# Sample tokens through ScalarE's DMA queue, sums of x held behind x, and separate banks for the second value tile, in a hybrid mLSTM and attention layer

## Chip, cores and metric

One core of one Trainium2 chip. The metric is the device time of one execution in microseconds (us). Engines: PE is TensorE (matmuls and transposes; PEld its weight loads), DVE is VectorE, ACT is ScalarE, POOL is GpSimd, SP is SyncE, which issues most DMAs. 0.3% of this kernel's time is 7.5 us.

## The reference

One inference step of one decoder layer. 512 prompt tokens and 32 sample tokens (8 sequences of 4), each a row of 2048 numbers, go through the same layer:

```
u = x @ w_in                      # 2048 x 18952, split into q,k,v,o,z (mLSTM), q,k,v,z (attention), two gates, ig, fg
h_m = mlstm(q_m, k_m, v_m, ig, logsigmoid(fg))      # 4 heads of 512, with a carried state C, n, m
h_a = sliding_window_attention(q_a, k_a, v_a)       # 32 heads of 64 over 4 key/value heads, window 128, sinks
br_m = norm(h_m) * sigmoid(o_m) * silu(z_m);  br_a = h_a * silu(z_a)
y = sigmoid(g_m) * (br_m @ w_proj_m) + sigmoid(g_a) * (br_a @ w_proj_a)
out = layernorm(2**0.25 * x + y @ w_out)
```

All is float32. Besides `out` for both groups of tokens, the new states C, n, m and the new key and value buffers are returned.

## The kernel before

**Products.** The 544 tokens (512 + 32) are the columns of the moving operand, in two halves of 272; 128 columns of a weight are the stationary one. A float32 product is made of three products in the faster fp32r form: a number is split into a high part (a cast to fp32r by ScalarE) and a low part (the difference, by VectorE), and high times high, high times low and low times high are summed. `split` (L190 to L198) does this for a loaded weight half, 128 partitions of 8 × 128: `wh` on ScalarE, `wl` on VectorE. `hilo` (L237) does it for x. A weight half is a tile `raw`, loaded by `load_half` (L185) on SP's queue, and `wh` and `wl` have two buffers each.

**Plain tiles.** `gemm` (L219) makes one block of 128 output columns from 16 blocks k of 128 rows of x: 16 × 3 × 2 = 96 products (L205) into two PSUM banks of the pool `bank` (4 buffers). Only the attention's value columns, two such blocks `VA_` (kk = 0 and 1, L572 to L583), are made so, and the gates' 8 columns (`gates_half`, L364 to L382, twice 32 products at L381). The gates' halves stand before each half of kk = 1.

**Paired tiles.** All later blocks go two at a time through `paired` (from L643), a scheme in the manner of Strassen and Winograd: seven products of quarter size in place of eight. Each step has 24 products (16 with `wh`, L643, and 8 with `wl`, L645), and one of seven moving operands: quadrants of x (`a11`, `xk`) or sums of quadrants (`s1`, `n2`, `n3`, `s4`), each as a high and a low tile (`s1h`, `s1l` and so on). `prepare` adds raw weight quadrants (L623, on VectorE) and splits them, three steps ahead; `gather` takes results out of the banks into `ev` tiles.

**The start.** After a first load of constants come 20 warm-up transposes (L288). x is loaded by SP in five pieces of 256, 256, 512, 512 and 512 columns (L296), with weight halves of the value tiles between them. The sample tokens (`xs`, L302) are two loads of 32 × 1024 on SP's queue, behind the second piece of x and the first weight half. The loop from L310 takes the 16 blocks k: 4 transposes (L315) into a tile of the pool `sm` (4 buffers), whose contents are then cast and differenced into `a11`, `a21` (k below 8) or `xk` (k from 8). At k = 2 the sample tokens are turned too, in 16 transposes of 32 × 32 (L319) into one tile `pxs`, which is read out after every second pair of blocks (L332 to L338). For k below 8 ScalarE also copies the block into `n2r` and `s1r` (L323, L324); for k from 8 VectorE subtracts the copy from the new block (L328, and L338 for the sample tokens): this makes s1. n3 is formed at L342. `x_sums` (L538 to L562) then does the rest: n2 = n2r − s1r in four chunks (L541), `hilo` of n3, s1 and n2 in four chunks each, and, once the plain tiles are done, s4. Each chunk is 128 × 544.

**Order.** Each engine runs its instructions in one fixed order. A scheduler chooses that order when the kernel is built, from a simulated timeline in which each instruction has an estimated cost; `tc.high_priority` moves instructions ahead, and `tc.issue_after(ins)` holds an instruction behind `ins` on the engine that runs `ins`. Side work (`x_sums`, gates, `attn_values`) is written as generators, taken a step further at every `tick()`.

```
for kk in range(2):
    ps = gemm(win, VA_ + kk * 128, xh, xl, ..., every=4, prio=500 * kk, before=gates_between if kk else None)
    if kk == 0:
        sums_ = x_sums(); spawn(sums_); gates_ps = mm()
```

With four `bank` buffers, kk = 0 holds two and the gates two, so that kk = 1 gets its two when ScalarE has copied out those of kk = 0 (`ev`, L582).

Of the kernel before, what the change touches and what calls it, by code (L numbers as in the profile page):

```python
# [15 lines left out]
F32 = mybir.dt.float32  # L16
F32R = mybir.dt.float32r
AF = mybir.ActivationFunctionType
ALU = mybir.AluOpType

D = 2048
SEQ = 512
NB = 8
NTS = 4
NS = NB * NTS
T = SEQ + NS
KT = D // 128
# [46 lines left out]
def _build(tc, nc, i, o, es):  # L74
# [11 lines left out]
    V, A, G, PE = nc.vector, nc.scalar, nc.gpsimd, nc.tensor  # L86
# [13 lines left out]
    def nm(s):  # L100
        count[0] += 1
        return f"{s}_{count[0]}"

    def sm():
        return psB.tile([128, 512], F32, tag="sm", name=nm("sm"))
# [4 lines left out]
    def r32(ap):  # L110
        return ap.bitcast(F32)
# [4 lines left out]
    def blk(ap, n=4):  # L116
        return ap.rearrange("p (b x) -> p b x", b=n)
# [7 lines left out]
    state = {}  # L125
# [17 lines left out]
    ident = cc[:, C_ID:C_ID + 128]  # L143
# [41 lines left out]
    def load_half(wv, c0, half):  # L185
        raw = wr.tile([128, 8, 128], F32, tag="raw", name=nm("raw"))
        load_part(raw, wv, c0, half)
        return raw

    def split(raw, p=None, tags=("wh", "wl"), parts=1):  # L190
        p = p or wp
        wh = p.tile([128, 8, 128], F32R, tag=tags[0], name=nm("wh"))
        wl = p.tile([128, 8, 128], F32R, tag=tags[1], name=nm("wl"))
        n = 8 // parts
        for k in range(0, 8, n):
            A.copy(wh[:, k:k + n], raw[:, k:k + n])  # L196
            V.tensor_tensor(out=wl[:, k:k + n], in0=raw[:, k:k + n], in1=r32(wh[:, k:k + n]), op=ALU.subtract)  # L197
        return wh, wl  # L198
# [11 lines left out]
    EVEN = ((0, 0, 272), (1, 272, 272))  # L210

    def bank():
        return psA.tile([128, 512], F32, tag="bank", name=nm("bank"))

    def mm():

        return [bank(), bank()]

    def gemm(wv, c0, xh, xl, cols=EVEN, raws=(None, None), every=8, prio=0, before=None, parts=(1, 1)):  # L219
        ps = mm()  # L220
        for half in range(2):
            if before:
                before(half)
            raw = raws[half] or load_half(wv, c0, half)
            if prio:
                with tc.high_priority(offset=prio):
                    wh, wl = split(raw, parts=parts[half])
            else:
                wh, wl = split(raw, parts=parts[half])
            products(ps, half, wh, wl, xh, xl, cols, every)  # L230
        return ps
# [5 lines left out]
    def hilo(src, hi, lo, eng=None):  # L237
        A.copy(hi, src)
        (eng or V).tensor_tensor(out=lo, in0=src, in1=r32(hi), op=ALU.subtract)
# [10 lines left out]
    HT = T // 2  # L250
# [14 lines left out]
    xh, xl = xview(0), xview(1)  # L265
# [4 lines left out]
    wr2 = pool(esQ, "wr2", 3)  # L270
# [7 lines left out]
    n2r = tx.tile([128, 8, HT], F32, name="n2r")[:]  # L278
    s1r, n3r = (act2.tile([128, 8, HT], F32, tag="act", name=nm("r"))[:] for _ in range(2))

    def two_k(ch):
        return slice(ch * 2, ch * 2 + 2)

    xs_src = i["x_sample"].rearrange("b t d -> (b t) d")
    xp_src = i["x_prompt"][0].rearrange("(t p) d -> p t d", p=128)
    warm = sm()
    for _ in range(20):
        PE.transpose(warm[:, 0:128], ident, ident)  # L288
    raw0, xt, xs = [], [], []
    for c0, n in ((0, 256), (256, 256), (512, 512), (1024, 512), (1536, 512)):  # L290
        if c0 < 1536:
            t_ = xr.tile([128, 4, n], F32, tag=f"x{n}", name=nm("xr"))[:]
        else:
            t_ = act2.tile([128, 8, HT], F32, tag="act", name=nm("xr"))[:].rearrange("p a b -> p (a b)")
            t_ = blk(t_[:, 0:4 * n])
        xdma = nc.sync.dma_start(t_, xp_src[:, :, c0:c0 + n])  # L296
        xt += [t_[:, :, c:c + 128] for c in range(0, n, 128)]
        if c0 == 256:
            raw0.append(load_half(win, VA_, 0))
            for c in range(0, D, 1024):  # L300
                xs_ = wr2.tile([128, 8, 128], F32, tag="raw2", name=nm("xs"))
                nc.sync.dma_start(xs_[:NS].rearrange("p a b -> p (a b)"), xs_src[:, c:c + 1024])  # L302
                xs += [xs_[:NS, q] for q in range(8)]
        elif c0 == 1024:
            raw0.append(load_half(win, VA_, 1))
    state["load"] = xdma
# [2 lines left out]
    pxs = sm()  # L309
    for g in range(8):  # L310
        for q in range(2):
            k = g * 2 + q
            pt = sm()
            for t in range(4):
                PE.transpose(pt[:, t * 128:t * 128 + 128], xt[k][:, t], ident)  # L315
            if k == 2:

                for k_ in range(KT):
                    PE.transpose(pxs[:, k_ * 32:k_ * 32 + 32], xs[k_], ident[:NS, :NS])  # L319
            if k < 8:  # L320
                hilo(pt[:, 0:HT], a11[0][:, k], a11[1][:, k])
                hilo(pt[:, HT:SEQ], a21[0][:, k, 0:SEQ - HT], a21[1][:, k, 0:SEQ - HT])
                A.copy(n2r[:, k], pt[:, 0:HT])  # L323
                A.copy(s1r[:, k, 0:SEQ - HT], pt[:, HT:SEQ])  # L324
            else:
                hilo(pt[:], xk2[0][k // 4 - 2][:, k % 4, 0:SEQ], xk2[1][k // 4 - 2][:, k % 4, 0:SEQ])
                c = (slice(None), k - 8, slice(0, SEQ - HT))
                V.tensor_tensor(out=s1r[c], in0=pt[:, HT:SEQ], in1=s1r[c], op=ALU.subtract)  # L328
        if g % 2:
            k4 = slice((g // 2) * 4, (g // 2) * 4 + 4)  # L330
            src = blk(pxs[:, k4.start * 32:k4.stop * 32])
            if g < 4:  # L332
                hilo(src, *(a21[p][:, k4, SEQ - HT:HT] for p in range(2)))
                A.copy(s1r[:, k4, SEQ - HT:HT], src)
            else:
                hilo(src, *(xk2[p][g // 2 - 2][:, :, SEQ:T] for p in range(2)))
                c = (slice(None), slice(k4.start - 8, k4.stop - 8), slice(SEQ - HT, HT))
                V.tensor_tensor(out=s1r[c], in0=src, in1=s1r[c], op=ALU.subtract)  # L338
        if g == 3:
            for ch in range(4):  # L340
                ks_ = two_k(ch)
                V.scalar_tensor_tensor(n3r[:, ks_], n2r[:, ks_], -1.0, s1r[:, ks_], op0=ALU.mult, op1=ALU.subtract)  # L342
# [182 lines left out]
    def attn_keys(kk, kt):  # L525
# [9 lines left out]
        nc.sync.dma_start(kb_p[0].rearrange("t k d -> t (k d)")[:, cs], kr[:, 0:128])  # L535
        nc.sync.dma_start(d_ks[:, cs], kr[:32, 128:256])

    def x_sums():  # L538
        for ch in range(4):
            ks_ = two_k(ch)  # L540
            V.tensor_tensor(out=n2r[:, ks_], in0=n2r[:, ks_], in1=s1r[:, ks_], op=ALU.subtract)  # L541
            if ch % 2:
                yield
        for name, r_ in (("n3", n3r), ("s1", s1r), ("n2", n2r)):
            h_, l_ = S[name] = quad(act2, name)
            for ch in range(4):
                ks_ = two_k(ch)
                hilo(r_[:, ks_], h_[:, ks_], l_[:, ks_])
                if ch % 2:
                    yield  # L550

        while not state.get("plain_done"):
            yield
        s4 = S["s4"] = quad(act, "s4")
        for ch in range(4):
            ks_ = two_k(ch)
            k0 = (ch * 2) % 4
            h12, l12 = (r32(xk2[p][ch // 2][:, k0:k0 + 2, 0:HT]) for p in range(2))
            V.tensor_tensor(out=n2r[:, ks_], in0=h12, in1=n2r[:, ks_], op=ALU.subtract)
            V.tensor_tensor(out=n2r[:, ks_], in0=n2r[:, ks_], in1=l12, op=ALU.add)  # L560
            hilo(n2r[:, ks_], s4[0][:, ks_], s4[1][:, ks_])
            yield  # L562
# [8 lines left out]

    for kk in range(2):  # L572
        ps = gemm(win, VA_ + kk * 128, xh, xl, raws=((raw0[0], raw0[1]), (raw0[2], None))[kk], every=4, prio=500 * kk,
                  before=gates_between if kk else None)
        if kk == 0:
            sums_ = x_sums()
            spawn(sums_)
            gates_ps = mm()
        vt = ev()
        with ahead_of_sums():  # L580
            for p_, v_ in halves(ps, vt):
                A.copy(v_, p_)  # L582
        spawn(attn_values(kk, vt))  # L583
# [873 lines left out]
    for ct in range(16):  # L1457
        sg = c5t()
        nc.sync.dma_start(sg[:], d_sga[ct])
        ps = gemm(wa_, ct * 128, bah, bal, every=2)  # L1460
# [3 lines left out]
        if bmh is None and (not live or ct == 15):  # L1464
# [8 lines left out]
            wr2, pe_ = pool(esR, "wr2b", 3), pool(esR, "peb", 1)  # L1473
# [99 lines left out]
    wr2, pe_ = pool(esR, "wr2d", 3), pool(esR, "ped", 1)  # L1573
# [3 lines left out]
    for ct in range(4):  # L1577
        ps = gemm(wo, ct * 128, yh, yl, every=4, prio=AHEAD)
# [168 lines left out]
    raws = [load_half(wo, ct * 128, half) for ct, half in ((12, 0), (12, 1), (13, 0))]  # L1747
# [12 lines left out]
    ps = gemm(wo, 12 * 128, yh, yl, cols=CUT, prio=AHEAD, raws=raws[:2])  # L1760
# [5 lines left out]
    for g in range(G3):  # L1766
        ct = 16 - G3 + g
        ps = sm()
        raws = [raws[2] if (g, half) == (0, 0) else load_half(wo, ct * 128, half) for half in range(2)]
# [66 lines left out]
```

## Time and profile before

| | us |
|---|---|
| median of 3 runs | 2510.77 (2508.2 to 2514.76) |
| profiled execution, own time | 2505.34 |
| its span in the trace | 2503.5 |
| mean granted clock of PE | 0.996 |

The profile is of one execution. Its page begins with each engine's busy time and share. Other views ask the trace for more: a table by stretches of time; the groups of like instructions; the waits of an engine, with the engine, line and tile that ended them; and the timeline, whose rows give the start, the duration, the engine, the line, the operation, output<-inputs with their shape and the count, and in brackets the idle time before the row and what ended it. The duration of a matmul row reaches to its modelled end, which overlaps the next; the distance between starts is what a matmul costs.

### The profile page before, as it was taken

How to read it: one execution, taken by the hardware profiler on the slowest of the kernel's cores; microseconds unless marked ns; L12 is line 12 of the kernel's file. 1: busy time of each engine (PE TensorE's matmuls, PEld its weight loads, DVE VectorE, ACT ScalarE, POOL GpSimd, SP SyncE). 2: the span in 40 equal slices, each digit the busy share in tenths (PEclk: the TensorE clock that was granted, in tenths of full speed). 3: DMA queues.
4: the chain of work that ended last, by engine and by line, in shares of the span. 5: the costliest groups of instructions: out<-in, count | busy, mean ns of one | idle time of the engine just before them, and what ended most of it. 6: DMA issues, size and time to landing. Idle time of an engine off the chain costs nothing.

```text
span 2503.5 us, 48635 instructions
## 1 busy us (share of the span) xinstructions
PE 2476.5 (99%) x19562; PEld 2413.9 (96%) x19562; DVE 1814.0 (72%) x2783; ACT 1240.0 (50%) x2026; POOL 383.5 (15%) x370
## 2 busy tenths in 40 slices
PE   8999999999999999999999999999999999999997
PEld 8999999999999999999999999999999999999997
DVE  7867777777677677887777778777866654767667
ACT  5457676677677665443433444444633323344431
POOL 0211211211121120221112122211000000110101
PEclk9999999999999999999999999999999999999999
DMA  6776666666666645467576566566755546788776
GB/s 169 179 186 156 152 150 165 149 152 166 149 147 164 155 116 146 118 209 229 174 222 216 170 202 213 177 212 217 246 179 166 183 141 211 209 230 258 213 217 194
DMA packets 551089, 457.35 MB, mean 183 GB/s; under 512 B 44784, under 2 KB 451232, under 8 KB 550576
## 3 DMA queue, kind: packets, MB, share of 16 engines
q1 hardware_dynamic: 534160, 394.99, 52.7%
q0 software_dynamic: 15696, 57.15, 11.7%
q8 instruction: 154, 2.52, 0.4%
q10 hardware_dynamic: 1008, 2.10, 0.2%
q14 instruction: 71, 0.58, 0.1%
HBM read 313.82 MB, written 94.22 MB: 163 GB/s over the span
## 4 chain that ended last, share of the span: by engine, by line
PE 90%; issue 4%; DMA 2%; DVE 2%; ACT 0%; POOL 0%; SPq 0%; DVEq 0%; POOLq 0%; ACTq 0%
PE bank L643 45%; PE bank L645 22%; PE bank L205 9%; PE sm L1340 2%; PE sm L1159 1%; PE sm L1153 1%; PE sm L1372 1%; PE sm L751 1%; PE sm L1385 1%; PE sm L789 1%; PE sm L779 1%; PE sm L1702 1%; DMA raw<-in_w_out 1%; DMA raw<-in_w_in 0%; DVE wl L197 0%
## 5 line engine op out<-in xcount | busy, mean ns | idle before, releaser
L196 ACT CAST wh<-raw 128x1024 fp32r<-128x1024 f32 x632 | 661.9, 1048 | 822.8 <-PE bank L643 675.4
L197 DVE TENSOR_TENSOR wl<-raw,wh 128x1024 fp32r<-128x1024 f32 x632 | 780.6, 1236 | 266.9 <-ACT wh L196 226.5
L643 PE MATMUL bank<-xk,wh 128*128 128x272 f32 x2336 | 321.8, 288 | 0.7 <-DVE ev L668 0.7
L623 DVE TENSOR_TENSOR raw<-raw,raw 128x1024 f32<-128x1024 f32 x238 | 302.3, 1272 | 10.3 <-DMA raw<-in_w_in 4.9
L643 PEld LDWEIGHTS bank<-xk,wh 128*128 128x128 f32 x2336 | 303.6, 188 | 4.3 <-ACT wh L196 2.1
L662 POOL TENSOR_TENSOR ev<-p,ev 128x272 f32<-128x272 f32 x82 | 122.3, 1491 | 608.8 <-ACT ev L661 536.6
L645 PE MATMUL bank<-xk,wl 128*128 128x272 f32 x1168 | 173.5, 288 | 0.0
L643 PE MATMUL bank<-s1h,wh 128*128 128x272 f32 x656 | 170.0, 290 | 0.7 <-ACT wh L196 0.7
L643 PE MATMUL bank<-n3l,wh 128*128 128x272 f32 x656 | 169.6, 290 | 0.0
L643 PE MATMUL bank<-s4h,wh 128*128 128x272 f32 x656 | 169.3, 289 | 0.1
L643 PE MATMUL bank<-n3h,wh 128*128 128x272 f32 x656 | 169.3, 289 | 0.0
L643 PE MATMUL bank<-n2l,wh 128*128 128x272 f32 x656 | 169.0, 290 | 0.0
L643 PE MATMUL bank<-s1l,wh 128*128 128x272 f32 x656 | 168.8, 290 | 0.0
L643 PE MATMUL bank<-n2h,wh 128*128 128x272 f32 x656 | 168.7, 288 | 0.0
L643 PE MATMUL bank<-s4l,wh 128*128 128x272 f32 x656 | 168.6, 290 | 0.0
L645 PEld LDWEIGHTS bank<-xk,wl 128*128 128x128 f32 x1168 | 156.8, 188 | 0.1
L643 PE MATMUL bank<-a11l,wh 128*128 128x272 f32 x584 | 150.1, 290 | 0.0
L643 PE MATMUL bank<-a11h,wh 128*128 128x272 f32 x584 | 149.9, 288 | 0.0
L205 PE MATMUL bank<-bh,wl 128*128 128x272 f32 x704 | 148.2, 289 | 0.4 <-DVE wl L197 0.4
L205 PE MATMUL bank<-bh,wh 128*128 128x272 f32 x704 | 147.8, 290 | 0.0
L205 PE MATMUL bank<-bl,wh 128*128 128x272 f32 x704 | 147.3, 288 | 0.0
L621 POOL DMA_DIRECT2D raw<-raw x90 | 78.1, 868 | 310.6 <-DVE sums L764 153.1
(460 smaller groups left out, 5622.3 us busy)
## 6 DMA issues: line engine op xcount, KB each, us to landing
raw<-in_w_in SPq DMA_DIRECT2D x296, 512.0 KB, 4.3
raw<-raw POOLq DMA_DIRECT2D x90, 512.0 KB, 4.9
C<-in_state_mlstm_C SPq DMA_DIRECT2D x32, 1024.0 KB, 5.6
out<-C SPq DMA_DIRECT2D x64, 512.0 KB, 3.5
raw<-in_w_proj_a SPq DMA_DIRECT2D x32, 512.0 KB, 4.5
raw<-in_w_proj_m SPq DMA_DIRECT2D x32, 512.0 KB, 4.2
raw<-in_w_out SPq DMA_DIRECT2D x32, 512.0 KB, 4.6
d_sgm<-ev SPq DMA_DIRECT2D x16, 272.0 KB, 5.7
```

The source lines that it names most:

```text
L196: A.copy(wh[:, k:k + n], raw[:, k:k + n])
L197: V.tensor_tensor(out=wl[:, k:k + n], in0=raw[:, k:k + n], in1=r32(wh[:, k:k + n]), op=ALU.subtract)
L205: PE.matmul(ps[f][:, :w], a[:, kk], b(k, c, w), start=(k == 0 and n == 0), stop=(k == 15 and n == 2))
L621: G.dma_start(out=w[out][:], in_=w[b][:], accum_op=ALU.add)
L623: V.tensor_tensor(out=w[out][:], in0=w[a][:], in1=w[b][:], op=ALU.add)
L643: PE.matmul(ps, wh[:, k], x(p, k), start=(first and k == 0 and p == 0), stop=False, skip_group_check=True)
L645: state["end"] = PE.matmul(ps, wl[:, k], x(0, k), start=False, stop=(k == 7), skip_group_check=True)
L662: G.tensor_tensor(out=c22, in0=p1, in1=c11, op=ALU.subtract)
L751: PE.matmul(pp[:, c0 + w0:c0 + 256], qs[a][:, j * 128:j * 128 + 128], kx[:, k0:k0 + 256 - w0], start=(n == 0), stop=(n == 1))
L779: PE.transpose(pt[:, (m - m0_) * 128:(m - m0_) * 128 + 128], s_[:, b, 128:256] if own else s_[:, b + 1, 0:128], ident)
L789: PE.matmul(po[:, b * 128:b * 128 + n], VA[:, b], p_[:, 2 * b:2 * b + n // 128], start=(b == 0 and m == 0), stop=(b == 3 and m == 1), skip ...
L1340: PE.matmul(pp[:, 0:258], a[:, b * 128:b * 128 + 128], b_[:, b, f], start=(b == 0 and n == 0), stop=(b == 3 and n == 2))
```

## The change

1. The sample tokens are loaded by four DMAs of 32 × 512 that ScalarE's queue issues ahead of everything, each into 32 partitions of one 128 × 512 tile. They are turned in 4 transposes of 128 × 128 instead of 16 of 32 × 32; `pxs` is the same afterwards except for the order of its columns, which the reads from it follow.
2. The last subtraction of L328 (the end of x) is remembered, and in `x_sums` the subtraction of n2 and the `hilo` of n3, s1 and n2 are put behind it by `issue_after`. As that instruction is VectorE's, this binds the VectorE parts (n2, and the low tiles); ScalarE's casts are not bound.
3. The second value tile (kk = 1) accumulates in two `sm` tiles in place of two `bank`s.

```diff
-    def gemm(wv, c0, xh, xl, cols=EVEN, raws=(None, None), every=8, prio=0, before=None, parts=(1, 1)):
-        ps = mm()
+    def gemm(wv, c0, xh, xl, cols=EVEN, raws=(None, None), every=8, prio=0, before=None, parts=(1, 1),
+             ps=None):
+        ps = ps or mm()
...
-    raw0, xt, xs = [], [], []
+    raw0, xt = [], []
+    xs = wr2.tile([128, 8, 128], F32, tag="raw2", name=nm("xs"))
+    for q in range(4):
+        nc.scalar.dma_start(xs[q * 32:q * 32 + 32, 0:4].rearrange("p a b -> p (a b)"), xs_src[:, q * 512:q * 512 + 512])
...
-            for c in range(0, D, 1024):
-                xs_ = wr2.tile([128, 8, 128], F32, tag="raw2", name=nm("xs"))
-                nc.sync.dma_start(xs_[:NS].rearrange("p a b -> p (a b)"), xs_src[:, c:c + 1024])
-                xs += [xs_[:NS, q] for q in range(8)]
...
             if k == 2:
-                for k_ in range(KT):
-                    PE.transpose(pxs[:, k_ * 32:k_ * 32 + 32], xs[k_], ident[:NS, :NS])
+                for c in range(4):
+                    PE.transpose(pxs[:, c * 128:c * 128 + 128], xs[:, c], ident)
...
-                V.tensor_tensor(out=s1r[c], in0=pt[:, HT:SEQ], in1=s1r[c], op=ALU.subtract)
+                state["x_end"] = V.tensor_tensor(out=s1r[c], in0=pt[:, HT:SEQ], in1=s1r[c], op=ALU.subtract)
...
-            src = blk(pxs[:, k4.start * 32:k4.stop * 32])
+            src = pxs[:].rearrange("p (c q t) -> p q c t", c=4, q=4)[:, g // 2]
...
+    def behind_x():
+        return tc.issue_after(state["x_end"].ins)
...
-            V.tensor_tensor(out=n2r[:, ks_], in0=n2r[:, ks_], in1=s1r[:, ks_], op=ALU.subtract)
+            with behind_x():
+                V.tensor_tensor(out=n2r[:, ks_], in0=n2r[:, ks_], in1=s1r[:, ks_], op=ALU.subtract)
...
-                hilo(r_[:, ks_], h_[:, ks_], l_[:, ks_])
+                with behind_x():
+                    hilo(r_[:, ks_], h_[:, ks_], l_[:, ks_])
...
-                  before=gates_between if kk else None)
+                  before=gates_between if kk else None, ps=[sm(), sm()] if kk else None)
```

## Prediction

> **What bounds the kernel now.** I read the page's head first, then the table by stretches, cut where the start ends.
>
> ```profile
> span 2503.5 us, 48635 instructions
> PE 2476.5 (99%) x19562; PEld 2413.9 (96%) x19562; DVE 1814.0 (72%) x2783; ACT 1240.0 (50%) x2026; POOL 383.5 (15%) x370
> ```
>
> ```profile
> 0.00:110.00 110.00, 100.61 (x739) 96.57 (x740) 91.37 (x160) 58.86 (x120) 15.47 (x22) 0.97 0.64 162
> 110.00:2503.50 2393.50, 2375.92 (x18825) 2317.38 (x18824) 1722.60 (x2624) 1181.12 (x1907) 368.08 (x348) 1.00 0.65 184
> ```
>
> A row of the second view is a stretch, its length, the busy time (and count) of PE, PEld, DVE, ACT and POOL, the granted clock, the DMA share and GB/s. After 110 us PE is busy 2375.92 of 2393.50, and one instruction takes 2375.92/18825 = 0.126 us: nothing but fewer products would shorten that part. The order of the instructions written for the changed kernel is the same on PE from its 970th instruction or so, which is at about 110 us. So the change decides at most the first 110 us, of which PE lacks 110.00 − 100.61 = 9.4. Two stretches of those tell more:
>
> ```profile
> 18.56:41.86 23.30, 21.16 (x153) 18.78 (x151) 22.65 (x47) 18.09 (x46) 1.85 (x2) 1.00 0.61 140
> 41.86:110.43 68.57, 66.16 (x518) 64.77 (x518) 64.58 (x102) 34.09 (x54) 13.31 (x15) 1.00 0.57 139
> ```
>
> While x comes in (up to 41.86, the end of the last difference of L328), VectorE is busy 22.65 of 23.30. From there to 110.43 (the `wl` difference of the second step of the third pair) it is busy 64.58 of 68.57, idle 3.99. So VectorE carries the whole start, and PE follows it closely. That decides this change: VectorE work that is put off is not gone. What PE waits for in the start:
>
> ```profile
> PE sm L319 <- DMA xs<-in_x_sample: 2.2, 1, 2.2
> PE bank L205 <- DVE xk L239: 1.2, 1, 1.2
> PE bank L643 <- ACT wh L196: 0.7, 1, 0.7
> PE bank L205 <- ACT ev L582: 0.5, 1, 0.5
> PE bank L205 <- DVE a21l L239: 0.5, 1, 0.5
> PE bank L205 <- DVE wl L197: 0.3, 1, 0.3
> ```
>
> **Part 1, the sample tokens.** The timeline of the start:
>
> ```profile
> 2.75 1.47 SPq L302 DMA_DIRECT2D xs<-in_x_sample  x2
> 6.95 1.89 PE L315 MATMUL sm<-cc,xr 128*128 128x128 f32 x12
> 10.32 1.04 ACT L196 CAST wh<-raw 128x1024 fp32r<-128x1024 f32 x1 [8.29 <-DMA raw<-in_w_in]
> 11.05 1.77 PE L319 MATMUL sm<-cc,xs 32*128 32x32 f32 x16 [2.21 <-DMA xs<-in_x_sample]
> 12.75 0.59 PE L205 MATMUL bank<-a11h,wh 128*128 128x272 f32 x1
> 16.82 0.43 PE L205 MATMUL bank<-a21h,wl 128*128 128x272 f32 x1
> 17.05 1.96 PE L315 MATMUL sm<-cc,xr 128*128 128x128 f32 x12
> 32.12 0.37 PE L381 MATMUL bank<-a11h,wga 128*128 128x272 f32 x1
> 36.20 1.04 PE L315 MATMUL sm<-cc,xr 128*128 128x128 f32 x8
> ```
>
> PE stands 2.21 us for the sample tokens, then transposes them 1.7 us (11.05 to 12.75), and only then starts on products, though `wh` is there at 10.32 + 1.04 = 11.36. In the changed kernel four DMAs ahead of everything on ScalarE's queue replace SP's two, and 4 transposes the 16. At x's pitch (1.96/12, at most 0.16 us) four take 0.65 and fit between 8.84 (6.95 + 1.89) and 11.36. The first product can then start at 11.36, 1.4 earlier; `wh` is what is late next. The order of the changed kernel puts 13 products ahead of the transposes of block 3, not 18: at the pitch here, (16.82 − 12.75)/17 = 0.24, that is 11.36 + 13 × 0.24 = 14.5, plus some 0.4 for the row that starts the bank; I take 14.9, so 17.05 − 14.9 = 2.1 earlier. Against it stand the bytes: 32 tokens × 8 KB = 0.26 MB now ride ahead of x and the first weight half, where they stood behind the latter. At 373 GB/s (the row below) that is 0.7 us if they delay all of it, 0 if they fit into the start-up. I take 0.3, so this part moves the front by 1.8, with 0 (the transfer binds) and 2.1 as ends. On SP the third x load must wait for a completion counter of the first sample piece; the two x loads and the weight half ahead of it are 1.5 MB, 4 us of transfer, so I cost that at nothing; if a sample piece landed late it would cost what it is late.
>
> [...]
>
> The clock:
>
> ```profile
> 11.00:12.00 1.00, 0.95 (x10) 0.98 (x11) 0.60 (x1) 1.00 (x4) 0.00 (x0) 0.61 1.03 373
> 17.00:18.00 1.00, 1.00 (x7) 1.00 (x6) 0.00 (x0) 0.00 (x0) 0.00 (x0) 0.50 1.07 370
> 18.00:19.00 1.00, 1.00 (x10) 0.93 (x8) 0.44 (x1) 0.78 (x3) 0.00 (x0) 0.98 1.04 381
> ```
>
> The granted clock falls to half right after the 2.21 us wait and is back at 18 us. The forecast leaves it so, since 11.36 still follows some 2 us of idling (from 9.5). If it stayed full, 13 products of 0.125 instead of 0.24 would save 1.5 more: a rival below. [...]
>
> **Part 2, sums behind x.** Only the VectorE halves are held by `issue_after`; ScalarE's casts stay free. What leaves the stretch before 41.86, and its pitch:
>
> ```profile
> L239 DVE TENSOR_TENSOR n3l<-r,n3h 128x544 fp32r<-128x544 f32 x4 | 2.9, 723 | 0.1
> L541 DVE TENSOR_TENSOR n2r<-n2r,r 128x544 f32<-128x544 f32 x3 | 2.2, 726 | 0.0
> L239 DVE TENSOR_TENSOR s1l<-r,s1h 128x544 fp32r<-128x544 f32 x3 | 2.1, 733 | 0.0
> ```
>
> ```profile
> 36.28 1.37 DVE L239 TENSOR_TENSOR s1l<-r,s1h 128x544 fp32r<-128x544 f32 x2
> 37.55 0.73 DVE L541 TENSOR_TENSOR n2r<-n2r,r 128x544 f32<-128x544 f32 x1
> ```
>
> Two in a row step by (37.55 − 36.28)/2 = 0.635, so ten are 6.35 us. VectorE's own work for x is then 22.65 − 6.35 = 16.3; from 18.56 − 1.8 = 16.76 it could end at 33.1. But the last transposes of x (block 15) stand on PE behind the 32 gate products, in both orders. Before, these end at 36.20. In the changed order PE does from 14.9 to there: 61 products × 0.125 = 7.6 (one steps by (36.20 − 32.12)/32 = 0.1275), 49 transposes × 0.11 (of the row at 36.20: (1.04 − 0.29)/7) = 5.4, 32 gate products 4.0: 31.9 without a stall. Before, the same account from 18.76 to 32.12 (50 products, 33 transposes: 9.9 of 13.4) left 3.5 of stalls, behind VectorE for the most part. With 6.35 less there I keep half, 1.6, and take 33.5 (ends 31.9 and 35.4). Behind that come a transpose, on ScalarE the cast of the second tile's `wh` (1.05), the cast and difference of `xk`, 0.6 each, and L328's, 0.4: x ends at about 36.7, against 41.86: 5.2 earlier.
>
> On PE, from the gates' end to the first product of L643, the changed order has 150 products and 9 transposes (before: 156 and 13): 18.75 + 1.0, plus 0.9 for stalls (0.3 for `wl`, which stays, and restarts; the 1.2 for `xk` goes) = 20.7, so L643 starts at 54.2, not
>
> ```profile
> 60.18 0.29 PE L643 MATMUL bank<-a11h,wh 128*128 128x272 f32 x1
> 108.84 0.39 PE L643 MATMUL bank<-s1h,wh 128*128 128x272 f32 x1 [0.74 <-ACT wh L196]
> ```
>
> 60.18. **PE's lead is 6.0 us, but VectorE has to follow.** The ten operations now come after x_end: 64.58 + 6.35 = 70.9 of work up to what was 110.43. Idle there was 3.99; most is waiting for `wh` and PE:
>
> ```profile
> L197 DVE TENSOR_TENSOR wl<-raw,wh 128x1024 fp32r<-128x1024 f32 x17 | 20.5, 1209 | 3.1 <-ACT wh L196 2.1 <-PE bank L205 0.9
> ```
>
> A VectorE that is behind its feeders does not wait for them; I keep 1.0 (a weight load that SP issues behind the value rows' writes; ends 0 and 3.99). 36.7 + 70.9 + 1.0 = 108.6, against 110.43: **1.8 us earlier**. PE's lead of 6.0 shrinks to that in waits for `wl` and for `s1l`, `n2l`, `n3l` and `s4` before 110 us; after that PE is the bound and the 1.8 stays. So of what the change brings to the front, about two thirds are given back.
>
> **Part 3, own banks.** The second value tile no longer waits for the first one's eviction: of the 0.5 us for `ev` L582 above, all goes. It lies on PE ahead of L643, so it is in the 20.7 and is given back with it: nothing of its own. Two of the four `sm` tiles are then held to the tile's end; the value transposes need one at a time. Lacking one would cost at most an eviction, some 0.5.
>
> Sum: 2505.34 − 1.8 = 2503.5 for the profiled execution (its span 2503.5 and 1.84 around it). That execution is 5.43 below the shown median of 2510.77 (2508.2 to 2514.76), so against the median it is **2509.0**.
>
> **Rivals.** *Full gain:* the late work finds gaps, because the reciprocal
>
> ```profile
> 65.13 3.54 DVE L411 RECIPROCAL t<-t 4x544 f32<-4x544 f32 x1
> ```
>
> and the gate rows around it are not needed by PE's products and slip behind the `wl` differences. VectorE without waits from 33.1: 33.1 + 70.9 = 104.0, 6.4 earlier; PE's lead of 6.0 then bounds: 2504.8. For it: the order does place the reciprocal later than before. Against: it is VectorE work of the same stretch.
>
> *Clock:* it stays full, 1.5 more at the front, and VectorE, which has 36.7 − 33.1 = 3.6 of slack there, passes it on: 2507.5.
>
> *Nothing:* the sample bytes delay x and the weight as much as the wait cost, or the scheduler's pinning only exchanges stalls: 2510.8. For it: the DMA share is 1.03 from 11 us on.
>
> *Slower:* ScalarE at the third pair. The changed order has 49 table loads instead of 45, all four new ones around the gates' exponentials at the third pair, in front of casts of `wh`.
>
> ```profile
> L1213 ACT ACT_TABLE_LOAD x6 | 7.7, 1283 | 0.1
> ```
>
> 4 × 1.283 = 5.1 us, and the exponentials stand in ScalarE's queue waiting for VectorE's gate rows. Already PE waits there for `wh` (108.84, 0.74 us). If the loads come one by one between casts, ScalarE's idle half (34.09 busy of 68.57) hides them. It decides as soon as VectorE's rows come over 3 us later than the order supposed: then 5.1 land on PE, less the 1.8, +3.3, and up to +8 if casts queue for the rows besides: 2514 to 2519.
>
> **How the numbers follow.** Forecast 0.45 (2509.0, own range 2507 to 2510.5), full gain 0.20, clock 0.08, nothing 0.12, slower 0.15. The range from 2502.0 (the full gain, less the 0.7 us at 108.84 if that wait goes too, less 2.1 for the median's own spread: the lowest run shown is 2.57 below it) to 2514.0 (the low end of the slower case) leaves out most of the slower case and a little of the full gain, some 0.17. A difference of 0.3%, 7.5 us, is about what a measurement of this kernel can tell from none. Only the far end of the full gain reaches it on one side, the far end of the slower case and mishaps at the table loads on the other: faster 0.15, same 0.73, slower 0.12.
>
> **What would show it.** First product near 11.4, block 3's transposes near 14.9, no wait of PE on the sample tokens (part 1). Last L328 near 36.7 and first L643 near 54 (part 2). Then new waits of PE on `wl` or the sums' low halves between 54 and 110 us, some 4 us in all, which would show the giving back; without them the full gain holds. No PE wait on `ev` L582 (part 3). PE waiting on `wh` at the third pair with table loads ahead of it would show the slower rival. Most likely wrong is how much of VectorE's put-off work really stands ahead of PE's needs: that step alone decides between 1.8 and 6.

## Result and the profile after

The changed kernel takes 2513.73 us (median of 11 runs, 2509.74 to 2516.96), the kernel before 2507.34 (11 runs, 2504.23 to 2514.76). The ratio is 1.0026, interval [1.0018, 1.0033]: some 6.5 us slower. The forecast was 1.8 us faster. It is within 0.3%, but the sign was wrong, and clearly so.

The head of the changed kernel's page, and the stretch after 110 us in both kernels (changed kernel first, then the one before; columns as in the prediction):

```profile
span 2511.9 us, 48616 instructions
PE 2476.6 (99%) x19550; PEld 2412.4 (96%) x19550; DVE 1811.2 (72%) x2783; ACT 1245.3 (50%) x2030; POOL 385.7 (15%) x370
```

```profile
0.00:110.00 110.00, 97.67 (x723) 92.78 (x724) 88.43 (x148) 57.02 (x114) 13.76 (x22) 1.00 0.62 162
110.00:200.00 90.00, 85.85 (x666) 84.56 (x666) 56.71 (x94) 52.92 (x85) 12.06 (x12) 0.98 0.75 184
```

```profile
110.00:200.00 90.00, 90.00 (x723) 89.81 (x722) 59.55 (x88) 52.38 (x86) 12.15 (x12) 1.00 0.79 199
```

PE is busy as long as before (2476.6 against 2476.5), in a span 8.4 longer: the loss is idle time. Up to 110 us PE is 2.9 less busy than before (100.61), from 110 to 200 another 4.2. That second row is where the prediction took PE to be bound and any gain to be safe.

**A measure that is finer than the time.** The order of products is the same in both kernels from about 110 us on, so one can ask when the same product starts. The first product of the sixth pair, changed kernel and kernel before:

```profile
178.93 0.29 PE L649 MATMUL bank<-a11h,wh 128*128 128x272 f32 x1
```

```profile
171.41 0.29 PE L643 MATMUL bank<-a11h,wh 128*128 128x272 f32 x1
```

It lags by 7.52 us. The table loads of ScalarE, which stand all through the kernel up to 1804 us, lag by the same 7.5 up to 926 us and by 6.6 from 963 us on. So nearly all of it is lost before 171 us; 1.0 comes back between 926 and 963 us, and near 2160 us another 1.4 is lost. At that last place VectorE waits for a weight load (`raw<-in_w_proj_m`), 1.45 us in the profiled execution of the kernel before, 2.70 in the changed one and 5.96 in `parts1_3` below, whose lag grows by 6.6 there; with one execution of each it is not shown whether that goes with the edits, and it is one source of scatter that the times have and the lag at 171 us does not. For each kernel below I give this lag, against the kernel before, at four products: the first paired one (60.18 in the kernel before), the first s1 product of the third pair (108.84), a xk product of the fourth (138.22), and 171.41. Minus is earlier.

| kernel | 60.18 | 108.84 | 138.22 | 171.41 | ratio of times, interval |
|---|---|---|---|---|---|
| changed kernel | −4.40 | +0.50 | +4.47 | +7.52 | 1.0026 [1.0018, 1.0033] |
| part1_alone | −3.05 | −1.32 | −1.07 | +1.70 | 1.0007 [0.9998, 1.0017] |
| part2_alone | −2.77 | +1.18 | +5.19 | +7.36 | 1.0027 [1.0016, 1.0038] |
| part3_alone | −1.57 | +2.54 | +4.09 | +4.66 | 1.0007 [0.9998, 1.0016] |
| exps_late | −5.02 | +0.47 | +0.80 | +7.56 | 1.0035 [1.0022, 1.0047] |
| parts1_3 | −5.13 | −1.23 | +0.68 | +1.74 | 1.0012 [1.0003, 1.0022] |
| after_light | −4.74 | −1.44 | −1.43 | −0.19 | 1.0001 [0.9992, 1.0010] |
| before_light | −1.10 | −0.54 | −0.49 | −0.13 | 1.0006 [0.9996, 1.0016] |
| copies_elsewhere | −4.80 | −2.92 | +1.37 | +3.84 | 1.0025 [1.0013, 1.0037] |
| copies_deferred | −4.69 | +0.17 | +4.21 | +5.31 | 1.0029 [1.0019, 1.0039] |
| three_waits | −4.72 | −3.42 | −3.07 | −0.03 | 1.0003 [0.9995, 1.0012] |
| three_waits_unpinned | −4.64 | −5.92 | −6.01 | −2.79 | 0.9991 [0.9982, 1.0000] |
| before_three | −1.04 | −0.31 | −0.32 | −0.30 | 1.0000 [0.9990, 1.0009] |

The ratios follow the last column within about 3 us, with intervals of some 2.5 us to either side; the lag is of one profiled execution each. How much executions differ at the front can be seen from `before_light` and `before_three`, which leave the front as it was and still start the first paired product 1.0 to 1.1 us earlier, with the granted clock at half for 3.41 us there and not for 6.83. So about 1 us of each lead in the first column can be that one execution; by 171 us these two differ by 0.3 or less. Around 138 us transposes stand at other places between the products, which moves single readings there by up to 1 us.

So the changed kernel does start its paired products 4.4 us earlier. Then it loses 4.9 up to the third pair and 7.0 more behind it. Of PE's waits from 0 to 160 us:

```profile
PE bank L649 <- ACT wh L196: 6.8, 6, 2.9
PE bank L649 <- DVE ev L674: 1.6, 1, 1.6
PE bank L205 <- ACT wh L196: 1.3, 1, 1.3
PE bank L649 <- DVE ev L670: 0.8, 1, 0.8
```

The waits for the sample tokens, for `xk` and for the eviction of the first value tile are gone. In their place PE waits six times for a cast of `wh`, and for evictions by VectorE (line numbers are 6 higher than before). The places, in order of time, first the front:

```profile
9.43 0.60 PE L319 MATMUL sm<-cc,xs 128*128 128x128 f32 x4
...
11.33 0.39 PE L205 MATMUL bank<-a11h,wh 128*128 128x272 f32 x1 [1.30 <-ACT wh L196]
...
14.33 0.60 PE L316 MATMUL sm<-cc,xr 128*128 128x128 f32 x4
...
30.80 0.37 PE L381 MATMUL bank<-a11h,wga 128*128 128x272 f32 x1
...
35.96 1.23 DVE L197 TENSOR_TENSOR wl<-raw,wh 128x1024 fp32r<-128x1024 f32 x1 [3.26 <-ACT wh L196]
...
37.71 0.40 DVE L328 TENSOR_TENSOR r<-sm,r 128x240 f32<-128x240 f32 x1
...
55.78 0.29 PE L649 MATMUL bank<-a11h,wh 128*128 128x272 f32 x1
```

then the stretch of VectorE that held the prediction's sum (end of x to the same `wl` of the third pair), and the two rows in it where VectorE stood idle:

```profile
38.11:113.24 75.13, 67.08 (x520) 64.99 (x518) 70.19 (x108) 36.67 (x55) 11.60 (x15) 1.00 0.55 135
```

```profile
77.37 0.28 DVE L520 COPY ev<-sm 32x128 f32<-32x128 f32 x1 [2.96 <-DMA out<-ev]
...
101.94 1.23 DVE L197 TENSOR_TENSOR wl<-raw,wh 128x1024 fp32r<-128x1024 f32 x1 [1.54 <-ACT wh L196]
```

and the three places where PE loses most, each with what stands in front of it:

```profile
80.64 2.28 PE L649 MATMUL bank<-xk,wh 128*128 128x272 f32 x16 [1.62 <-DVE ev L674]
...
93.88 1.49 POOL L668 TENSOR_TENSOR ev<-p,ev 128x272 f32<-128x272 f32 x1 [8.89 <-DMA d_ks<-ev]
95.32 0.87 POOL L627 DMA_DIRECT2D raw<-raw  x1
...
100.86 1.99 ACT L196 CAST wh<-raw 128x1024 fp32r<-128x1024 f32 x2 [5.06 <-DMA raw<-raw]
102.91 0.39 PE L649 MATMUL bank<-a11h,wh 128*128 128x272 f32 x1 [1.68 <-ACT wh L196]
...
109.30 1.28 ACT L474 ACT_TABLE_LOAD   x1
110.60 0.66 ACT L474 ACTIVATE t<-t 4x544 f32<-4x544 f32 x1
111.16 0.37 ACT L659 ACTIVATE p<-bank 128x272 f32<-128x272 f32 x1
111.54 1.28 ACT L1219 ACT_TABLE_LOAD   x1
112.83 0.66 ACT L1219 ACTIVATE ev<-ev 128x544 f32<-128x544 f32 x1
113.39 1.03 ACT L196 CAST wh<-raw 128x1024 fp32r<-128x1024 f32 x1
114.47 0.60 PE L649 MATMUL bank<-n2h,wh 128*128 128x272 f32 x1 [2.85 <-ACT wh L196]
```

They read as three chains. At 80 us a bank is not evicted, because VectorE, which evicts, stood 2.96 us at a copy into an `ev` tile until a store (`out`) had landed. This is the copy of the second value tile's sample rows, and VectorE is not late there. The store was issued at 73.25, against 74.34 in the kernel before; but the copy stands earlier in VectorE's order, where the kernel before has it behind more weight and gate rows and an eviction. The same row in the kernel before, in `part1_alone` and in `parts1_3` (both below, and neither with anything pinned):

```profile
78.96 0.27 DVE L520 COPY ev<-sm 32x128 f32<-32x128 f32 x1
```

```profile
76.43 0.28 DVE L520 COPY ev<-sm 32x128 f32<-32x128 f32 x1 [2.81 <-DMA out<-ev]
```

```profile
73.61 0.28 DVE L520 COPY ev<-sm 32x128 f32<-32x128 f32 x1 [2.97 <-DMA out<-ev]
```

`part2_alone` and `part3_alone` wait 3.00 and 2.92 us there. So this wait comes with any of the three parts alone. At 102 us the copies of the keys, which VectorE makes behind that stand (at 89.43, against 86.72 before), make the store `d_ks` late; that store holds the `ev` tile that GpSimd waits for; behind GpSimd's operation stands the DMA that accumulates one weight quadrant onto another (`raw<-raw`, L627); `wh` waits for that, and PE for `wh`. At 114 us two table loads, an exponential, an eviction and a sigmoid fill ScalarE from 109.30 to 113.39, ahead of the cast that PE needs. VectorE's gate rows come late for them: L445 at 108.83, against 101.17 before, and L471 at 111.95, against 104.28. From 114 to 118 us the granted clock is 0.61 and 0.53, too.

### The profile page after: what moved, and what is told of

The parts are those of the page before. It is cut to its first block, busy times and chain, and to the rows that moved or that the text cites. A ratio compares the mean times of both kernels' runs of the same rounds, so it can differ in the third digit from the quotient of the medians.

```text
span 2511.9 us, 48616 instructions
## 1 busy us (share of the span) xinstructions
PE 2476.6 (99%) x19550; PEld 2412.4 (96%) x19550; DVE 1811.2 (72%) x2783; ACT 1245.3 (50%) x2030; POOL 385.7 (15%) x370
## 4 chain that ended last, share of the span: by engine, by line
PE 96%; DMA 1%; ACT 1%; DVE 1%; issue 0%; POOL 0%; SPq 0%; DVEq 0%; ACTq 0%; POOLq 0%
PE bank L649 45%; PE bank L651 22%; PE bank L205 13%; PE sm L1346 2%; PE sm L1165 1%; PE sm L1159 1%; PE sm L1378 1%; PE sm L205 1%; PE sm L757 1%; PE sm L1391 1%; PE sm L795 1%; PE sm L785 1%; PE sm L1708 1%; DMA raw<-in_w_in 0%; DMA raw<-raw 0%; ACT wh L196 0%
## 5 line engine op out<-in xcount | busy, mean ns | idle before, releaser
L649 PEld LDWEIGHTS bank<-n2h,wh 128*128 128x128 f32 x656 | 124.3, 190 | 4.7 <-ACT wh L196 4.4
```

The lines of the kernel that those rows point to most:

```text
L649: PE.matmul(ps, wh[:, k], x(p, k), start=(first and k == 0 and p == 0), stop=False, skip_group_check=True)
```

## Experiments

Theories, as the expectations name them. A: the pinned sums come late on VectorE, and the exponentials with their table loads behind them; they cost the loss. A2: the sharper form, that pinning leaves VectorE idle while the gates run and its ready work comes later. Rivals: B, the early sample bytes delay x; C, the own banks are at fault; D, the backlog of VectorE alone, so that table loads do not matter; D2, weights and accumulating DMAs are late by themselves; E, any lead is lost to later waits, whoever makes it; F, a wait taken away moves to the next late row; G, the copies of the old buffers hold up the accumulating DMAs.

**Each part alone.** `part1_alone` (the other two undone), `part2_alone` and `part3_alone` are cut from the changed kernel by these edits:

```diff
 # pinning undone
-        return tc.issue_after(state["x_end"].ins)
+        return ExitStack()
 # own banks undone
-                  ..., ps=[sm(), sm()] if kk else None)
+                  ...)
 # sample tokens undone: loads, transposes and reads as in the kernel before
```

> Part 1 alone: the sample tokens through ScalarE's queue, nothing pinned, value tile in banks; the written order keeps 45 table loads with the four exponentials together. Theory A (put-off VectorE work and, behind it, the exponentials with four extra table loads cost the 6.5 us; the front itself is a gain): no put-off work here, so the front's gain of 2 to 3 us stays or is half given back: 1 to 3 us faster than before, PE never waits for the sample tokens, clock full from 11 us. Rival B (the early bytes delay x and the weights): 0 to 3 us slower.

> Part 2 alone: the VectorE parts of the sums pinned behind x; the written order has 49 table loads, the exponentials between the sigmoids of the second pair. Theory A: this part carries the loss, 5 to 9 us slower than before, with PE waits on wh of 2 us or more near the exponentials and waits on evictions by VectorE between 60 and 85 us. Rival C (the own banks are at fault): within 1 us of before.

> Part 3 alone: the second value tile in two sm tiles; the written order has 47 table loads, the exponentials together but behind the first sigmoid. Theory A: the 0.5 us wait for the bank goes, two more table loads on ScalarE: 0 to 2 us slower than before. Rival C (the own banks are at fault, sm tiles lacking): 4 us slower or more.

Measured: 1.0007, 1.0027 and 1.0007. Part 2 carries the loss, as A has it; C falls. Part 1 does not give the gain of A. Its time, some 1.8 us slower, lies in B's range, but B's mechanism does not hold, as its first paired product is 3.05 us earlier; that lead turns into a lag of 1.70 up to 171 us. Part 3 lags 4.66 in its profile, more than its time shows. PE waits in part 3 for an accumulating DMA at 103 us and behind the exponentials at 114 us (2.20 and 1.38 us). So each part alone makes a lead (that of part 3, 1.57, is little more than the 1.1 by which executions differ), and each loses it: that is E, and A does not explain it for parts 1 and 3. A share that all three have in common is the wait of VectorE for the `ev` tile shown above.

**Pinning taken out**, the rest kept (first edit above).

> Parts 1 and 3 without the pinning; 47 table loads. Theory A2 (the pinning leaves VectorE idle while the gates run and puts its ready work behind x; that late work costs the evictions, the weights' differences and the gate rows): about what parts 1 and 3 cost alone, 0 to 3 us slower than before, first L649 product near 56. Rival E (each lead at the front is lost to waits later, whoever makes it): 4 to 8 us slower.

Measured: 1.0012, some 3 us slower, with an interval that reaches over A2's range and E's; the lag, +1.74, tells more. The lead at the front is 5.13, larger than with the pinning (4.40). Its VectorE, while the gates run, against the row at 35.96 of the changed kernel:

```profile
32.55 0.39 DVE L328 TENSOR_TENSOR r<-sm,r 128x240 f32<-128x240 f32 x1
32.86 0.71 DVE L546 TENSOR_TENSOR n2r<-n2r,r 128x544 f32<-128x544 f32 x1
33.49 1.35 DVE L240 TENSOR_TENSOR s1l<-r,s1h 128x544 fp32r<-128x544 f32 x2
34.77 0.71 DVE L546 TENSOR_TENSOR n2r<-n2r,r 128x544 f32<-128x544 f32 x1
35.40 1.21 DVE L197 TENSOR_TENSOR wl<-raw,wh 128x1024 fp32r<-128x1024 f32 x1
...
38.68 0.39 DVE L328 TENSOR_TENSOR r<-sm,r 128x240 f32<-128x240 f32 x1
```

Where the pinned VectorE stands 3.26 us, this one does four sums. x ends at 39.07, against 38.11: the pinning buys 0.96 us there, which PE does not get, and pays with 5.8 us of lag at 171 us (7.52 − 1.74). That is A2; by the times alone, 1.0026 against 1.0012, the intervals still touch. The rest, a lead of 5.13 turned into a lag of 1.74, is E. Of this, 3.9 go before 108.84, with the wait of 2.97 for the `ev` tile.

**VectorE made lighter.** The same edit in the changed kernel and in the one before; it leaves out the reciprocal and four of the six rows of a polynomial, so the gates' logsigmoid is not computed:

```diff
-        V.reciprocal(dd, dd)
...
-        for c in (13, 11, 9, 7, 5, 3):
+        for c in (9, 5):
```

> The whole change, with VectorE's gate rows lightened: the reciprocal (3.54 us) and four of the six rows of L419 (4 x 0.70) are left out, so the gates' logsigmoid and what hangs on it are not computed; 6.3 us less on VectorE, as much as the pinning put off; 45 table loads. Theory A2: the lead is kept for the most part, 1 to 5 us faster than before. Rival D2 (weights and accumulating DMAs late by themselves, not VectorE): still 3 us slower than before or more.

> The kernel before with the same rows left out (reciprocal and four of the six rows of the polynomial; the gates' logsigmoid is not computed). PE waits for VectorE little there: 0 to 1.5 us faster than before by every theory; it tells how much of the lightened changed kernel's gain is the lightening alone.

Measured: 1.0001 and 1.0006. With 6.3 us less on VectorE the changed kernel loses its whole lag (from +7.52 to −0.19), while the kernel before gains 0.13. So the 7.5 hang on how much VectorE has to do, and D2 falls. But the edit also brings the exponentials back in front of the sigmoids, in 45 table loads; this run does not tell that apart from the rest. And no gain of 1 to 5 us appears: a lead of 4.74 still goes.

**The exponentials moved.**

```diff
-                A.activation(o_[:], o_[:], AF.Sigmoid)
+                state["sig", o_ is o1] = A.activation(o_[:], o_[:], AF.Sigmoid)
...
+        for _ in range(6):
+            yield
+        with tc.issue_after(state["sig", True].ins), tc.issue_after(state["sig", False].ins):
             A.activation(T2[0:4], mrow, AF.Exp, scale=-1.0)
             ... # the three others
```

The six yields move here from further down.

> The whole change, with the four exponentials of the gates made later and held on ScalarE behind both sigmoids of the third pair: together in one place, 47 table loads instead of 49, and VectorE's gate rows done before ScalarE asks for them. Theory A, its second half (exponentials and table loads in front of casts of wh cost about 5 of the 6.5 us): 1 to 3 us slower than before, about 5 faster than the changed kernel, the 2.85 us wait of PE on wh near 114 us gone. Rival D (VectorE's backlog alone; the wait only moves on): 5 to 7 us slower than before.

Measured: 1.0035, some 8.8 us slower: nearest to D and beyond its 5 to 7, but for another reason than D's. The place itself behaves as A has it. ScalarE and PE there:

```profile
110.46 0.65 ACT L1220 ACTIVATE ev<-ev 128x544 f32<-128x544 f32 x1
111.24 1.05 ACT L196 CAST wh<-raw 128x1024 fp32r<-128x1024 f32 x1
112.34 0.39 PE L650 MATMUL bank<-n2h,wh 128*128 128x272 f32 x1 [0.73 <-ACT wh L196]
...
154.36 0.62 ACT L239 CAST k<-s 128x512 fp32r<-128x512 f32 x1 [5.95 <-DMA s<-d_ka]
...
156.28 0.40 PE L650 MATMUL bank<-a11h,wh 128*128 128x272 f32 x1 [3.12 <-ACT wh L196]
```

The cast comes 2.15 earlier (111.24, not 113.39), PE waits 0.73 and not 2.85, and the lag at 138.22 is 0.80 instead of 4.47. Then 6.8 us are lost by 171 us: ScalarE stands for the keys that come back from memory (`s<-d_ka`), with a cast of `wh` behind it. About half of the 6.8 is that wait, and some 1.6 the clock behind it, which is at half for 3.41 us from 157 us on. A was right on the place and wrong on the whole: taking the wait away brought the next one (F).

**The copies out of the `ev` tiles.**

```diff
-        vr, vs = ev(512), ev(128)
+        vr, vs = t5(n=512), t5(n=128)
...
-        kr = ev(256)
+        kr = t5(n=256)
```

> The whole change, with the value and key copies (vr, vs, kr) in tiles of the gates' pool instead of the three ev tiles: VectorE's 2.96 us wait near 74 us for an ev tile held by a store should go, and POOL's 8.9 us wait for the d_ks store ahead of the accumulating DMA. Theory A2: 2 to 4 us of the loss go, so 2 to 5 us slower than before. Rival F (the waits only move to the next late VectorE row): 6 us slower than before or more.

Measured: 1.0025, time as F has it. The profile shows both waits gone, the step of 102.91 starting at 98.81 without a wait, and a lead of 2.92 at 108.84 where the changed kernel has a lag of 0.50. The copies of the keys come at 86.56 again, about where the kernel before has them. Behind it the exponentials cost 3.16 on `wh` (111.36 us) and later waits the rest.

**The copies of the old buffers deferred.**

```diff
-        with tc.issue_after(state["load"].ins):
-            ... # d_ks, d_vr and the old buffers to kb_s, vb_s
         for k in range(16):
...
+            if k == 6:
+                with tc.issue_after(state["load"].ins):
+                    ... # the same four DMAs
```

> The whole change, with only the copies of the old key and value buffers (L841, L842, 2 MB from memory to memory) and of the new rows issued at the sixth attention tile instead of near 128 us. Theory G (the accumulating DMAs of weights land 13 us late because those copies fill the DMA engines, and PE loses 2 to 3 us between 140 and 158): product at 158 us lags by 4 to 5.5 us instead of 7.5, time 3 to 5 us slower than before. Rival A2 alone (VectorE's lateness, whatever the DMAs do): lag stays above 6.5.

The lag is 5.30 at 158 us, where G asks for 4 to 5.5, and 5.31 at 171 us instead of 7.52; the time, 1.0029, is some 7.3 us slower and misses G's 3 to 5. The DMA view from 133 to 147 us, changed kernel and this one:

```profile
raw<-raw POOLq DMA_DIRECT2D x1, 512.0 KB, 13.3
raw<-in_w_in SPq DMA_DIRECT2D x1, 512.0 KB, 13.0
```

```profile
raw<-raw POOLq DMA_DIRECT2D x2, 512.0 KB, 4.7
```

The accumulating DMA landed 13.3 us after its issue behind the copies; without them the median of two was 4.7.

**All three waits taken away**: the last three edits together, on the changed kernel, on parts 1 and 3 without the pinning, and on the kernel before.

> The whole change with three waits taken away at once: exponentials behind the third pair's sigmoids, value and key copies outside the ev tiles, copies of the old buffers deferred. Theory (the front's lead of 4 to 5 us is eaten by these three waits behind VectorE's backlog): a lead of 1 to 4 us over the kernel before remains at 160 us, 1 to 4 us faster. Rival E (a chain of weight load, VectorE addition, accumulating DMA and cast sets the time whatever is taken away): lag between 0 and 5 us.

> The same three edits on parts 1 and 3, without the pinning. If the pinning is what makes VectorE late: 2 to 4 us faster than the kernel before, and ahead of the pinned version by 1 us or more. Rival E: lag between 0 and 3 us, as with parts 1 and 3 alone (1.7).

> The same three edits on the kernel before: what they are worth without the change. PE waits little there (1.5 us in all after 60 us) and two table loads are added: within 1.5 us of before.

Measured: 1.0003, 0.9991 and 1.0000. With the pinning the lead that was expected at 160 us is not there; without it the expectation of 2 to 4 us holds in the lag and, by some 2.3 us, in the time. The lead lives to 138 us: 3.07 with the pinning, 6.01 without. Then both lose 2 to 3 us between 147 and 153, again by the keys ahead of a cast of `wh`:

```profile
145.12 0.62 ACT L239 CAST k<-s 128x512 fp32r<-128x512 f32 x1 [5.42 <-DMA s<-d_ka]
...
145.95 1.04 ACT L196 CAST wh<-raw 128x1024 fp32r<-128x1024 f32 x1
147.04 0.39 PE L650 MATMUL bank<-a11h,wh 128*128 128x272 f32 x1 [1.43 <-ACT wh L196]
```

The rows are of the unpinned version. So without the three waits 7.55 of lag are gone (7.52 to −0.03), and the pinning costs 2.8 more even then: in the lag, and in the times of 11 runs each (2507.97 against 2505.14). The unpinned version is at 2505.14 us against 2507.50, faster than both kernels by its median and by its lead of 2.79, though its interval touches 1. The same edits are worth nothing on the kernel before, which has no lead to lose. The fourth wait, for the keys, was not tried.

## Why the prediction was wrong

**Part 1 was right, and its clock was not.** First product forecast at 11.4, measured 11.33; block 3's transposes at 14.9, measured 14.33. The granted clock stayed at 1.00, the rival given 0.08: PE's idling ahead of the first product was 1.30, not the 2 that I had counted. By that rival's own figures the transposes were then due at 13.4; a wait of 0.49 for `a21h` and smaller gaps took most of the difference. The traces show it halved behind waits of 2.21 (before) and 2.85 us (114 us here) and not behind 1.30. The bytes ahead of x do cost something: in all nine kernels with part 1 the first transposes of PE, which wait for the constants, start at 3.27 to 3.37, in the five without it at 2.63 to 2.77, and x's first transposes follow at 7.61 instead of 6.95. It is about the 0.7 us that I had named as the full price. It stays hidden, because PE waits for `wh` behind it all the same, and the first weight half is cast at 10.23, before at 10.32.

**The front came near.** The gates' end was forecast at 33.5 and came near 34.8 (`wh` cast behind it at 34.83); the end of x at 36.7, and came at 38.11; the first paired product at 54.2, and came at 55.78. A lead of 4.4 instead of 6.0, and that with the clock full, and against an execution of the kernel before that was some 1 us slower at the front than two others.

**The step that failed** is this: "A VectorE that is behind its feeders does not wait for them; I keep 1.0". VectorE's work in the stretch was sized well, 70.9 forecast, 70.19 measured. Its idle time was 4.94, beyond the upper end of 3.99 that I had named: 2.96 for an `ev` tile and 1.54 for `wh`. The first does not come from work that was put off, since parts 1 and 3 alone, with nothing pinned, have it too: the new order brings VectorE to a copy before the store has landed for which the copy waits. The second follows from it, as the rows above read: the copies of the keys come behind that stand, their store holds the tile of GpSimd, and GpSimd's accumulating DMA brings the weight late (`copies_elsewhere` takes the copies of values and of keys out of these tiles at once, so the two are not told apart). The stretch ended at 113.24, not 108.6: 2.8 behind the kernel before, where 1.8 ahead was forecast. Of these 4.6 the idle time is 3.9 and the end of x 1.4, with 0.7 less work against it.

**The second failure** is "after that PE is the bound and the 1.8 stays". PE is nearly always busy after 110 us in the kernel before (90.00 of 90.00 us up to 200); that does not say that the engines that feed it keep up when their rows come late. From 108.84 to 171.41 the changed kernel lost another 7.0.

**The slower rival was named, with its place and its price** (+3.3 to +8, at the table loads of the third pair, once VectorE's rows are over 3 us late) and given 0.15. The condition came true: VectorE's last gate rows were 7.7 us later than before (L471 at 111.95, against 104.28). That place cost 2.85 us of wait and some 1.7 of clock (4 us at 0.57); `exps_late` confirms it, with 3.7 of lag less at 138 us. It is about half of the loss; the other waits were not among the rivals.

**Part 3** took the wait of 0.5 us for the eviction away, and no lack of `sm` tiles shows in the waits. What it and part 1 gain is given back as well. The rivals "full gain" and "clock" took it that a gain stays; none stayed in any kernel that had not first been rid of the later waits, and 2.8 us of it in the one that was also rid of the pinning. Why the lead of 5 to 6 us is not kept there in full, beyond the wait for the keys, is open.

## What to carry to other kernels

When a change makes the start earlier, follow the next engine in the chain until the gain is safe, and ask of each of its rows what it must wait for, not of its busy time alone: a small copy that came up before a store had landed stopped VectorE for 3 us, with and without the work that was put off, and what stood behind it came late in turn. Holding ready work back so that an urgent chain goes first costs more than it brings where the engine then stands idle (3.26 us here, for 0.96). To see where a few microseconds go in 2500, compare the start of the same product in both traces: the lag is steady to hundredths from 178 to 926 us, where the times scatter by 10 us. But take a second execution of one kernel, as the front alone can differ by 1 us.

## What the runs showed of the hardware

The granted clock fell to half behind waits of PE of 2.21 us (kernel before) and 2.85 us (changed kernel, 114 us), and in `part2_alone` behind waits of 1.7 and 0.7 us (0.93 from 12 to 14 us, 0.50 from 14 to 16). It did not behind waits of 1.30 and 1.68 us in the changed kernel (at 11.33 and 102.91 us; 1.00 from 0 to 110). It stayed at half for 6.83 us in the kernel before (11.21 to 18.04) and for 3.41 us in the changed one (114.45 to 117.86): for a busy PE that is some 3.4 and 1.7 us, my estimate from these lengths and the 0.50. In the 3.41 us ahead of the fall PE was busy for 1.20 us in the kernel before and for 0.58 in the changed one; in the 3.41 us from 100.80 on, in the changed one, it was busy for 1.73 and the clock stayed at 1.00. The waits of 1.7 and 1.68 us are alike and had different outcomes, so the length of one wait does not decide it here; how much idling it takes is not shown. The 512 KB accumulating DMA issued at 133.30 us in the changed kernel landed after 13.3 us, behind 2 MB of copies from memory to memory issued from 128.53 us on; in `copies_deferred`, without the copies there, the median of two was 4.7. What is lost in the first 171 us of this kernel stays lost for long: the lag of ScalarE's table loads keeps at 7.5 us from 178 to 926 us. Sample tokens of 0.26 MB, issued ahead of everything on ScalarE's queue, go with constants that are there 0.6 us later (first transposes at 3.27 to 3.37 in nine kernels, 2.63 to 2.77 in five).
